# A decoder block on one core: pooling tiles behind all pairs' tiles, and an output projection in eight banks

## The chip, the cores and the metric

The kernel runs on one core of a Trainium2 chip. The metric is the device time of one execution in microseconds. A core has five engines with a queue each: TensorE (PE, matmuls; its weight loads are counted apart as PEld), VectorE (DVE), ScalarE (ACT), GpSimd (POOL), and SyncE (SP), which here issues every transfer between memory and the core. Matmuls write to PSUM, which has eight banks; one bank holds one 128x512 float32 tile.

## The reference

One decoder block on x of 512 tokens by 2048 channels. An adaLN vector (`mod`, six parts of 2048) shifts, scales and gates each half.

```
mod = silu(c) @ w_ada + b_ada                       # 6 x 2048
h   = rmsnorm(x) * (1 + sc1) + sh1
p   = h @ w_in                                      # 3360 RWKV columns + 1024 pooling columns
y_rwkv = rwkv7(p[:, :3360])                         # 16 heads of 64: r, k, v, decay, rate, gate
y_pool = pooling(p[:, 3360:])                       # 4 groups of 256, causal windows 2, 4, 8, 16, then a 256x256 matrix
x = x + gt1 * (concat(y_rwkv, y_pool) @ w_out)
x = x + gt2 * conv_ffn(rmsnorm(x) * (1 + sc2) + sh2)
out = rmsnorm(x)
```

In the pooling group with window w, each channel becomes its mean over the last w tokens minus itself, and the group's 256 channels are then mixed by one matrix. RWKV is a scan over tokens with a 64x64 state for each head.

## The kernel before

**Layout and tiles.** Activations lie transposed: 128 channels on the partitions, 512 tokens along the row. A product with a weight matrix is made of output tiles of 128 channels. For one tile, `project` (L122) loads the weights in blocks of 128x512 (four contraction steps of 128), splits each block into a high part (ACT, L112) and a low part (DVE, L114) and runs three matmuls for a step: high by high, high by low, low by high (`mm3`, L117; the profile's L118, L119, L120). A whole tile is 16 steps, 48 matmuls of 512 columns, accumulated in one PSUM bank. The activations are split in the same way into `ah` and `al` (`slots`, 16 pairs of homes); H, the first norm's output, lives in them, and later the 16 mixer outputs M.

**Stages.** First the norm and the first eight columns' tiles are built, while the first third of the adaLN rows is read. Then four quads follow, each two pairs of heads (four heads) of the RWKV mixer: `front(g)` (decay, rates, norm of k) and `rest(g)` (chunked scan: scores, a triangular inverse, eight chunk steps, group norm, gate). A quad is a long chain of small steps on PE, DVE and ACT, written under `hp()`, a higher priority. Around them stands the work that is to fill PE: `win_tile(fi)`, the remaining 27 tiles of the input projection. `win_pair(p, at)` makes the three tiles r, k and v of one pair, mixes each with its shifted self (`shift`, L232 and L233) and spills them to memory as `sp`; the quad loads them again (L693) when it starts. The tiles of the pooling columns (u tiles, two to a group) are spilled as `su` (L678 to L680).

**Order.** WIN_ORDER (L49) lays out the weights: three adaptor tiles, pairs 0 and 1, pairs 2 to 5, the eight pooling tiles, pairs 6 and 7. Pairs 2 and 3 are made under quad 0, pairs 4 and 5 under quad 1, the pooling tiles and pairs 6 and 7 under quad 2. Pooling itself (`pool(gi)`, L276), four groups in the order POOLS, is written behind quad 2 and has the high priority.

**Homes.** The order on each engine and the waits are set by a scheduler, by priority, by readiness in its own model of time, and by the homes of tiles. A tile name with one or two buffers is handed out again when its last user is done. Pooling borrows homes of the quads: K for the padded input, EM and EP for the running sums, INV for the result, AL for the output, and `war` (two buffers) for the pooling matrix. `war` is otherwise the home of the adaLN rows: `ada_rest` (L336) loads 96 blocks of 512 KB and multiplies each with silu(c) on DVE (L344), 24 written behind each quad. PSUM in this part: `mm` two banks (tiles and pooling), `bt` two by two banks and `ch` two banks (quads).

**Output projection.** Under quad 3 the first ten output tiles (NW) are made over the first 14 (NM) of 16 contraction steps: MIX_ORDER (L57) puts the eight pooling outputs first, then quads 0 to 2. The result, gated and added to x (L728), goes to memory as `part`. When quad 3 is done, all PSUM and working memory of this part are given back, and eight banks `b` are taken. `part` is loaded as x2 (L793), and the last two steps, quad 3's outputs, are added for the ten tiles. The six other tiles are made in two halves of 256 tokens each (`out_half`, L800), with the second norm behind them. The gated MLP follows; the change does not touch it.

The lines around the quads that the prediction speaks of:

Of the kernel before, what the change touches and what calls it, by code (L numbers as in the profile page):

```python
# [9 lines left out]
F32 = mybir.dt.float32  # L10
# [36 lines left out]

POOLS = (3, 1, 2, 0)
WIN_ORDER = ["T0", "T1", "T2", "r0", "k0", "v0", "r1", "k1", "v1"]  # L49
for _p in range(2, 6):  # L50
    WIN_ORDER += [f"r{_p}", f"k{_p}", f"v{_p}"]
WIN_ORDER += [f"u{2 * _g + _i}" for _g in POOLS for _i in range(2)]
for _p in range(6, NP):
    WIN_ORDER += [f"r{_p}", f"k{_p}", f"v{_p}"]


MIX_ORDER = [8 + 2 * _g + _i for _g in POOLS for _i in range(2)] + [0, 1, 2, 3, 4, 5, 6, 7]  # L57
NM = 14


# [1 line left out]
def block_kernel(ctx, tc, a, out, stop=None, dbg=None):  # L62
# [25 lines left out]
    def cols(name, lo, hi):  # L88
        return vec[:, COLS[name] + lo : COLS[name] + hi]
# [86 lines left out]
    if True:  # L176
# [53 lines left out]
        if True:  # L230
# [7 lines left out]
            def cell(tag, name):  # L238
                return ra.tile([P, WID.get(tag, 2 * T)], F32, tag=tag, name=name)

            def two(t):
                return t[:, 0 : 2 * T].rearrange("p (x t) -> p x t", x=2)
# [64 lines left out]
    def mmtile():  # L307
        return psa.tile([P, T], F32, tag="mm", name="mm", bufs=2)
# [7 lines left out]
    def win_tile(fi):  # L316
        ps = mmtile()
        project(ps, a["win1"][fi - 8, :, :], H)
        return ps
# [45 lines left out]
    def front(g, rkv):  # L365
        r, k, v = rkv
        lws = []
        for x in range(2):
            lw = ra.tile([P, 3, P], F32, tag="lw", name="lw", bufs=2)
            nc.sync.dma_start(lw, a["lora"][2 * g + x, :, :, :])  # L370
            lws.append(lw)

        def c2(name, x):
            return col(name, 2 * g + x)

        psw, psal = batch(), batch()
        for x in range(2):
            for m in range(2):
                PE.matmul(psw[HS[m], x, :], lws[x][0:64, 0, HS[m]], xwa[0:64, :], start=True, stop=True)
                PE.matmul(psal[HS[m], x, :], lws[x][64:128, 0, HS[m]], xwa[64:128, :], start=True, stop=True)  # L380
        sg = cell("EM", "sg")
        for x in range(2):
            S.activation(lead(sg)[:, NK * x : NK * x + NK, 1:], psw[:, x, :].rearrange("p (c t) -> p c t", t=C),
                         AF.Sigmoid, bias=c2("w0", x))
        V.memset(lead(sg)[:, :, 0:1], 0.0)
        al = cell("AL", "al")
        for x in range(2):
            act = S.activation(two(al)[:, x, :], psal[:, x, :], AF.Sigmoid, bias=c2("a0", x))
        with tc.issue_after(act.ins):
            act = S.preload_act_table_set("natural_log_exp_and_others")  # L390
        n = 2 * NK * (C + 1)
        V.tensor_tensor_scan(sg[:, 0:n], scanm[:, :, :].rearrange("p c t -> p (c t)"), sg[:, 0:n], 0.0,
                             op0=ALU.mult, op1=ALU.add)
        cs = lead(sg)
        mid = ra.tile([P, 2 * NK, 1], F32, tag="mid", name="mid")
        V.tensor_copy(mid, cs[:, :, C // 2 : C // 2 + 1])
        V.tensor_sub(cs, cs, mid[:, :, :].to_broadcast([P, 2 * NK, C + 1]))
        ep = cell("EP", "ep")
        em = sg
        fdec = ra.tile([P, 2 * NK, 1], F32, tag="fdec", name="fdec", bufs=2)  # L400
        with tc.issue_after(act.ins):
            S.activation(ep[:, 0:n], sg[:, 0:n], AF.Exp, scale=-Q)
            S.activation(em[:, 0:n], sg[:, 0:n], AF.Exp, scale=Q)
        V.tensor_mul(fdec[:, 0 : 2 * NK - 1], lead(ep)[:, 0 : 2 * NK - 1, C : C + 1], lead(em)[:, 1 : 2 * NK, 0:1])


        inv = cell("INV", "inv")
        psn = batch()
        for x in range(2):
            S.activation(two(inv)[:, x, :], two(k)[:, x, :], AF.Square, scale=c2("kk", x))  # L410
            PE.matmul(psn[:, x, :], bones, two(inv)[:, x, :], start=True, stop=True)
        V.tensor_scalar_max(flat(inv), wide(psn), 1e-24)
        with tc.issue_after(act.ins):
            S.activation(flat(inv), flat(inv), AF.Ln)
            S.activation(flat(inv), flat(inv), AF.Exp, scale=-0.5)
        for x in range(2):
            V.scalar_tensor_tensor(two(inv)[:, x, :], two(k)[:, x, :], c2("kk", x), two(inv)[:, x, :],
                                   op0=ALU.mult, op1=ALU.mult)
        return lws, al, ep, em, inv, fdec

    def rest(g, rkv, fr):
        r, k, v = rkv
# [234 lines left out]
    def win_pair(p, at):  # L657
        for i in range(3):
            ps = win_tile(at + i)
            t = ra.tile([P, T], F32, tag="spill", name="spill", bufs=2)  # L660
            shift(ps, 8 * i + p, t)
            d = tc.dram_tile([P, T], F32, name=f"sp{p}_{i}")
            nc.sync.dma_start(d, t)
            sp[p, i] = d

    def hp():
        return tc.high_priority(offset=100000)

    shift(win_tile(8), 17, two(rkv0[2])[:, 1, :])
    edge = []  # L670
    for g in range(NQ):
        if g < NQ - 1:
            if g == 2:
                for n, gi in enumerate(POOLS):
                    for i in range(2):
                        ps = win_tile(21 + 2 * n + i)
                        t = ra.tile([P, T], F32, tag="spill", name="spill", bufs=2)
                        S.copy(t, ps)  # L678
                        d = tc.dram_tile([P, T], F32, name=f"su{gi}_{i}")
                        nc.sync.dma_start(d, t)  # L680
                        su[gi, i] = d
            at = (9, 15, 29)[g]
            win_pair(2 * g + 2, at)
            win_pair(2 * g + 3, at + 3)
        with hp(), ExitStack() as after:
            for i in edge:
                after.enter_context(tc.issue_after(i.ins))
            rkv = rkv0
            if g:
                rkv = [cell(n, n.lower()) for n in RKV]  # L690
                for i in (1, 0, 2):
                    for x in range(2):
                        nc.sync.dma_start(two(rkv[i])[:, x, :], sp[2 * g + x, i])  # L693
            fr = front(g, rkv)
        with hp():
            rest(g, rkv, fr)
            if g == 2:
                for gi in POOLS:
                    edge = pool(gi)
        ada_rest(24 * g, 24 * g + 24)  # L700
        if g == 2:
            V.tensor_add(mod[:, 32:48], modq[:, 0, 0:16], modq[:, 1, 0:16])
            V.tensor_add(mod[:, 32:48], mod[:, 32:48], cols("b_ada", 32, 48))

    V.tensor_add(mod[:, 48:80], modq[:, 0, 16:48], modq[:, 1, 16:48])
    V.tensor_add(mod[:, 48:80], mod[:, 48:80], cols("b_ada", 48, 80))
    V.scalar_tensor_tensor(gsc2, mod[:, 64:80], 1.0, cols("n2", 0, 16), op0=ALU.add, op1=ALU.mult)


# [4 lines left out]
    def load_mix(i):  # L714
        t = wp.tile([P, WC], F32, tag="wraw", name="mxl", bufs=4)
        nc.sync.dma_start(t, mixd[MIX_ORDER[i]])
        M.append(split_act(i, t))

    for i in range(NM):
        load_mix(i)  # L720
    part = []
    for f in range(NW):
        if f % 2 == 0:
            xt = two(cell("K" if f % 4 == 0 else "R", "xt"))
            nc.sync.dma_start(xt, a["xT"][:, f : f + 2, :])
        ps = mmtile()
        project(ps, a["wout"][f, :, 0 : NM * P], M)
        V.scalar_tensor_tensor(xt[:, f % 2, :], ps, mod[:, 32 + f : 33 + f], xt[:, f % 2, :], op0=ALU.mult, op1=ALU.add)  # L728
        d = tc.dram_tile([P, T], F32, name=f"part{f}")
        nc.sync.dma_start(d, xt[:, f % 2, :])  # L730
        part.append(d)
    M += last_mix
    psctx.close()
    actx.close()

# [25 lines left out]
    def residual(f, ps, gate, acc, lo, hi, fresh):  # L761

        V.scalar_tensor_tensor(x2[f][:, lo:hi], ps, gate, x2[f][:, lo:hi], op0=ALU.mult, op1=ALU.add)
        sumsq(acc, x2[f][:, lo:hi], lo, hi, fresh)
# [22 lines left out]
            mm3(ups[i][:, hs], wh[:, sl], wl[:, sl], H2[k][0][:, hs], H2[k][1][:, hs], start=k == 0, stop=k == KT - 1)  # L787

    acc = rb.tile([P, T], F32, tag="acc", name="acc")
    x2 = []  # L790
    for f in range(KT):
        t = rb.tile([P, T], F32, tag=f"x2_{f}", name=f"x2_{f}")
        nc.sync.dma_start(t, part[f] if f < NW else a["xT"][:, f, :])  # L793
        x2.append(t)
    for f in range(NW):
        ps = bank()
        project(ps, a["wout"][f, :, NM * P :], M[NM:])
        residual(f, ps, mod[:, 32 + f : 33 + f], acc, 0, T, f == 0)

    def out_half(hf, f, engs=(V,)):  # L800
        ps = bank()[:, 0:HT]
# [225 lines left out]
```

## Time and profile before

| | |
|---|---|
| median of 3 runs | 2434.46 us |
| lowest, highest | 2431.72, 2441.41 us |
| profiled execution | 2428.03 us, span 2426.3 us |
| mean granted TensorE clock | 0.977 of full |
| PE, PEld busy | 2250.7 us (93%), 1825.1 us (75%) |
| DVE, ACT, POOL busy | 1344.6 us (55%), 817.7 us (34%), 27.3 us (1%) |
| moved | 357.05 MB, mean 147 GB/s |

The profile is of one execution. Its page gives the busy time of each engine, the span in 40 slices of 60.7 us (a digit is the busy share in tenths), and the costliest groups of instructions. Besides the page, the trace answers questions: a table by stage, a timeline of instructions, the sync queue's transfers, and who waited for whom. PE's busy time is modelled and overlapping matmuls are counted once; a few per cent of the matmul records can be missing.

### The profile page before, as it was taken

What the parts mean: (1) busy time and instruction counts of PE and PEld (TensorE: products, weight loads), DVE (VectorE), ACT (ScalarE), POOL (GpSimd) and SP (SyncE); (2) the same over time, 40 slices, a digit from 0 to 9 for tenths busy, and PEclk for the clock granted to TensorE, in tenths of its full rate; (3) what the DMA queues carried; (4) which work ended last, traced back from release to release, by engine and by line L of the source; (5) the groups of instructions that cost most, each with busy time, mean ns of one, the idle gap of its engine ahead of it and who ended that gap; (6) DMA issues with size and microseconds to landing.
All of it is one profiled execution on the core that took longest, in us unless ns stands there. A gap on an engine that the chain in (4) does not pass through costs nothing.

```text
span 2426.3 us, 36875 instructions
## 1 busy us (share of the span) xinstructions
PE 2250.7 (93%) x14434; PEld 1825.1 (75%) x14434; DVE 1344.6 (55%) x2230; ACT 817.7 (34%) x1349; POOL 27.3 (1%) x30
## 2 busy tenths in 40 slices
PE   4778899899857989999999999999999999999997
PEld 3656666678545779887888888888888888888887
DVE  7987784642496558657444433444344434444457
ACT  3242343332322346533223322333233323323333
POOL 0000000000000003000000000000000000000000
PEclk9989999999979999999999999999999999999998
DMA  9956762323577556447432333223322332332235
GB/s 358 339 208 209 239 190 82 96 89 122 188 237 247 179 200 202 144 156 256 127 99 97 96 97 99 96 96 96 99 96 97 97 98 96 96 100 96 96 101 174
DMA packets 186497, 357.05 MB, mean 147 GB/s; under 512 B 36305, under 2 KB 45265, under 8 KB 182097
## 3 DMA queue, kind: packets, MB, share of 16 engines
q1 hardware_dynamic: 186322, 354.69, 45.7%
q8 instruction: 113, 1.85, 0.3%
q14 instruction: 62, 0.51, 0.1%
HBM read 336.25 MB, written 18.36 MB: 146 GB/s over the span
## 4 chain that ended last, share of the span: by engine, by line
PE 74%; DVE 11%; DMA 9%; issue 3%; ACT 2%; SPq 1%; DVEq 0%; POOL 0%; ACTq 0%
PE b L118 20%; PE b L120 20%; PE b L119 20%; DMA war<-ada 4%; PE mm L120 4%; PE mm L118 4%; PE mm L119 3%; DVE jk L211 3%; DVE war L344 2%; DMA slot<-ada 1%; DVE wlo L114 1%; DMA wraw<-wup 1%; PE mm L298 1%; PE bt L561 0%; ACT ah L147 0%
## 5 line engine op out<-in xcount | busy, mean ns | idle before, releaser
L114 DVE TENSOR_TENSOR wlo<-wraw,whi 128x512 fp32r<-128x512 f32 (+1 forms) x782 | 534.9, 685 | 717.7 <-ACT whi L112 710.9
L112 ACT CAST whi<-wraw 128x512 fp32r<-128x512 f32 (+1 forms) x798 | 491.0, 616 | 1275.4 <-PE b L119 923.4
L120 PE MATMUL b<-hh,wlo 128*128 128x512 f32 (+1 forms) x1472 | 560.7, 381 | 7.2 <-DVE wlo L114 6.9
L118 PE MATMUL b<-hh,whi 128*128 128x512 f32 (+1 forms) x1472 | 559.9, 380 | 0.0
L119 PE MATMUL b<-hl,whi 128*128 128x512 f32 (+1 forms) x1472 | 559.6, 380 | 0.0
L118 PE MATMUL b<-ah,whi 128*128 128x512 f32 (+1 forms) x980 | 350.0, 357 | 4.5 <-ACT whi L112 3.5
L120 PE MATMUL b<-ah,wlo 128*128 128x512 f32 (+1 forms) x980 | 348.7, 356 | 4.7 <-DVE wlo L114 4.7
L119 PE MATMUL b<-al,whi 128*128 128x512 f32 (+1 forms) x980 | 348.5, 356 | 0.0
L120 PEld LDWEIGHTS b<-hh,wlo 128*128 128x128 f32 x1472 | 277.0, 188 | 62.6 <-DVE wlo L114 9.4
L118 PEld LDWEIGHTS b<-hh,whi 128*128 128x128 f32 x1472 | 277.1, 188 | 52.6 <-ACT whi L112 0.5
L119 PEld LDWEIGHTS b<-hl,whi 128*128 128x128 f32 x1472 | 277.1, 188 | 52.4
L118 PE MATMUL mm<-ah,whi 128*128 128x512 f32 x572 | 232.3, 406 | 10.7 <-ACT whi L112 10.7
L120 PE MATMUL mm<-ah,wlo 128*128 128x512 f32 x572 | 232.2, 406 | 4.9 <-DVE wlo L114 4.9
L119 PE MATMUL mm<-al,whi 128*128 128x512 f32 x572 | 230.2, 402 | 0.0
L118 PEld LDWEIGHTS b<-ah,whi 128*128 128x128 f32 x980 | 186.0, 190 | 34.1 <-ACT whi L112 6.0
L120 PEld LDWEIGHTS b<-ah,wlo 128*128 128x128 f32 x980 | 186.0, 190 | 31.4 <-DVE wlo L114 5.8
L119 PEld LDWEIGHTS b<-al,whi 128*128 128x128 f32 x980 | 186.1, 190 | 26.9 <-DVE al L141 1.2
L344 DVE SCALAR_TENSOR_TENSOR war<-war,cq 128x1024 f32<-128x1024 f32 x96 | 117.0, 1222 | 54.6 <-DMA war<-ada 53.9
L118 PEld LDWEIGHTS mm<-ah,whi 128*128 128x128 f32 x572 | 109.1, 191 | 38.7 <-ACT whi L112 11.5
L120 PEld LDWEIGHTS mm<-ah,wlo 128*128 128x128 f32 x572 | 109.0, 191 | 33.9 <-DVE wlo L114 8.9
L119 PEld LDWEIGHTS mm<-al,whi 128*128 128x128 f32 x572 | 109.1, 191 | 24.3 <-issue 1.7
L889 DVE SCALAR_TENSOR_TENSOR x<-b,mod,x 128x512 f32<-128x512 f32 x80 | 59.7, 751 | 111.7 <-PE b L120 111.7
(223 smaller groups left out, 1733.2 us busy)
## 6 DMA issues: line engine op xcount, KB each, us to landing
wraw<-wup SPq DMA_DIRECT2D x368, 256.0 KB, 3.0
war<-ada SPq DMA_DIRECT2D x96, 512.0 KB, 4.4
wraw<-wdn SPq DMA_DIRECT2D x192, 256.0 KB, 2.7
wraw<-win SPq DMA_DIRECT2D x140, 256.0 KB, 3.5
wa<-ada SPq DMA_DIRECT2D x32, 1024.0 KB, 7.1
wraw<-wout SPq DMA_DIRECT2D x78, 256.0 KB, 3.5
slot<-ada SPq DMA_DIRECT2D x64, 256.0 KB, 3.6
sp<-spill SPq DMA_DIRECT2D x18, 256.0 KB, 3.3
```

The lines of the kernel that those rows point to most:

```text
L112: S.copy(hi[:, 0:w], raw[:, 0:w])
L114: eng.tensor_tensor(lo[:, 0:w], raw[:, 0:w], hi[:, 0:w].bitcast(F32), op=ALU.subtract)
L118: PE.matmul(ps, wh, xh, start=start, stop=False)
L119: PE.matmul(ps, wh, xl, start=False, stop=False)
L120: return PE.matmul(ps, wl, xh, start=False, stop=stop)
L211: V.scalar_tensor_tensor(jk, wa, 1.0, cb, op0=ALU.mult, op1=ALU.mult, accum_out=mod[:, j : j + 1])
L298: pe = PE.matmul(ps, pw[:, i, d * P : (d + 1) * P], z[:, i, :], start=i == 0, stop=i == 1)
L344: V.scalar_tensor_tensor(wa, wa, 1.0, cq[0], op0=ALU.mult, op1=ALU.mult, accum_out=modq[:, kq, j : j + 1])
L889: V.scalar_tensor_tensor(x2[f], ps, mod[:, 80 + f : 81 + f], x2[f], op0=ALU.mult, op1=ALU.add)
```

## The change

- WIN_ORDER: the pairs 2 to 7 come first, the eight pooling tiles last. MIX_ORDER: quads 0 to 2, pooling, quad 3.
- Pairs 6 and 7 are made under quad 2; the pooling tiles under quad 3.
- `pool` is written behind quad 3's `rest`, with the order that it is issued behind the last load of quad 3's inputs and behind the last step of quad 3's `front`. The wait of a quad on pooling (`edge`) is dropped, and the inputs are loaded in the order r, v, k instead of k, r, v.
- The adaLN rows are summed once, for all of `mod[:, 32:80]`, behind the last quad.
- The partial output projection with its `part` tiles is dropped. When the eight banks are there, eight output tiles are made side by side in four blocks of four steps each (`out_block`); x is loaded as x2 during the third block row; the residuals follow; tiles 8 and 9 are made whole.

```diff
-for _p in range(2, 6):
+for _p in range(2, NP):
     WIN_ORDER += [f"r{_p}", f"k{_p}", f"v{_p}"]
 WIN_ORDER += [f"u{2 * _g + _i}" for _g in POOLS for _i in range(2)]
-for _p in range(6, NP):
-    WIN_ORDER += [f"r{_p}", f"k{_p}", f"v{_p}"]
-MIX_ORDER = [8 + 2 * _g + _i for _g in POOLS for _i in range(2)] + [0, 1, 2, 3, 4, 5, 6, 7]
+MIX_ORDER = [0, 1, 2, 3, 4, 5] + [8 + 2 * _g + _i for _g in POOLS for _i in range(2)] + [6, 7]
...
     for g in range(NQ):
         if g < NQ - 1:
-            if g == 2:
-                for n, gi in enumerate(POOLS):
-                    for i in range(2):
-                        ps = win_tile(21 + 2 * n + i)
-                        ...
-            at = (9, 15, 29)[g]
-            win_pair(2 * g + 2, at)
-            win_pair(2 * g + 3, at + 3)
-        with hp(), ExitStack() as after:
-            for i in edge:
-                after.enter_context(tc.issue_after(i.ins))
+            win_pair(2 * g + 2, 9 + 6 * g)
+            win_pair(2 * g + 3, 12 + 6 * g)
+        else:
+            for n, gi in enumerate(POOLS):
+                for i in range(2):
+                    ps = win_tile(27 + 2 * n + i)
+                    t = ra.tile([P, T], F32, tag="spill", name="spill", bufs=2)
+                    S.copy(t, ps)
+                    d = tc.dram_tile([P, T], F32, name=f"su{gi}_{i}")
+                    nc.sync.dma_start(d, t)
+                    su[gi, i] = d
+        with hp():
             rkv = rkv0
             if g:
                 rkv = [cell(n, n.lower()) for n in RKV]
-                for i in (1, 0, 2):
+                for i in (0, 2, 1):
                     for x in range(2):
-                        nc.sync.dma_start(two(rkv[i])[:, x, :], sp[2 * g + x, i])
-            fr = front(g, rkv)
-        with hp():
+                        load = nc.sync.dma_start(two(rkv[i])[:, x, :], sp[2 * g + x, i])
+            fr, norm = front(g, rkv)
             rest(g, rkv, fr)
-            if g == 2:
-                for gi in POOLS:
-                    edge = pool(gi)
+            if g == NQ - 1:
+                with tc.issue_after(load.ins), tc.issue_after(norm.ins):
+                    for gi in POOLS:
+                        pool(gi)
         ada_rest(24 * g, 24 * g + 24)
...
-    for i in range(NM):
-        load_mix(i)
-    part = []
-    for f in range(NW):
-        ...
-        project(ps, a["wout"][f, :, 0 : NM * P], M)
-        V.scalar_tensor_tensor(xt[:, f % 2, :], ps, mod[:, 32 + f : 33 + f], xt[:, f % 2, :], op0=ALU.mult, op1=ALU.add)
-        ...
-        part.append(d)
-    M += last_mix
     psctx.close()
     actx.close()
...
+    def out_block(f, k0):
+        return project(pss[f], a["wout"][f, :, k0 * P : (k0 + 4) * P], M[k0 : k0 + 4], start=k0 == 0, stop=k0 == KT - 4)
+
     x2 = []
-    for f in range(KT):
-        t = rb.tile([P, T], F32, tag=f"x2_{f}", name=f"x2_{f}")
-        nc.sync.dma_start(t, part[f] if f < NW else a["xT"][:, f, :])
-        x2.append(t)
-    for f in range(NW):
+    pss = [bank() for _ in range(8)]
+    for k0 in range(0, KT, 4):
+        for i in range(k0, min(k0 + 4, NM)):
+            load_mix(i)
+        if k0 == KT - 4:
+            M += last_mix
+        for f in range(8):
+            out_block(f, k0)
+            if k0 == 8:
+                for i in range(2):
+                    t = rb.tile([P, T], F32, tag=f"x2_{2 * f + i}", name=f"x2_{2 * f + i}")
+                    nc.sync.dma_start(t, a["xT"][:, 2 * f + i, :])
+                    x2.append(t)
+    for f in range(8):
+        residual(f, pss[f], mod[:, 32 + f : 33 + f], acc, 0, T, f == 0)
+    for f in range(8, NW):
         ps = bank()
-        project(ps, a["wout"][f, :, NM * P :], M[NM:])
-        residual(f, ps, mod[:, 32 + f : 33 + f], acc, 0, T, f == 0)
+        project(ps, a["wout"][f, :, :], M)
+        residual(f, ps, mod[:, 32 + f : 33 + f], acc, 0, T, False)
```

More of the change, by code (lines that the diff above doesn't have):

```diff
@@ L416, in front @@
         for x in range(2):
-            V.scalar_tensor_tensor(two(inv)[:, x, :], two(k)[:, x, :], c2("kk", x), two(inv)[:, x, :],
-                                   op0=ALU.mult, op1=ALU.mult)
-        return lws, al, ep, em, inv, fdec
+            norm = V.scalar_tensor_tensor(two(inv)[:, x, :], two(k)[:, x, :], c2("kk", x), two(inv)[:, x, :],
+                                          op0=ALU.mult, op1=ALU.mult)
+        return (lws, al, ep, em, inv, fdec), norm
     def rest(g, rkv, fr):
@@ L669, in block_kernel @@
     shift(win_tile(8), 17, two(rkv0[2])[:, 1, :])
-    edge = []
     for g in range(NQ):
         if g < NQ - 1:
-            if g == 2:
-                for n, gi in enumerate(POOLS):
-                    for i in range(2):
-                        ps = win_tile(21 + 2 * n + i)
[L677 to L681, printed above, removed]
-            at = (9, 15, 29)[g]
-            win_pair(2 * g + 2, at)
-            win_pair(2 * g + 3, at + 3)
-        with hp(), ExitStack() as after:
-            for i in edge:
-                after.enter_context(tc.issue_after(i.ins))
+            win_pair(2 * g + 2, 9 + 6 * g)
[10 more added lines that the diff above has]
+        with hp():
             rkv = rkv0
@@ L690, in block_kernel @@
                 rkv = [cell(n, n.lower()) for n in RKV]
-                for i in (1, 0, 2):
+                for i in (0, 2, 1):
                     for x in range(2):
-                        nc.sync.dma_start(two(rkv[i])[:, x, :], sp[2 * g + x, i])
-            fr = front(g, rkv)
-        with hp():
+                        load = nc.sync.dma_start(two(rkv[i])[:, x, :], sp[2 * g + x, i])
+            fr, norm = front(g, rkv)
             rest(g, rkv, fr)
-            if g == 2:
-                for gi in POOLS:
-                    edge = pool(gi)
+            if g == NQ - 1:
+                with tc.issue_after(load.ins), tc.issue_after(norm.ins):
+                    for gi in POOLS:
+                        pool(gi)
         ada_rest(24 * g, 24 * g + 24)
[L701 to L706, printed above, removed]
+    V.tensor_add(mod[:, 32:80], modq[:, 0, :], modq[:, 1, :])
+    V.tensor_add(mod[:, 32:80], mod[:, 32:80], cols("b_ada", 32, 80))
     V.scalar_tensor_tensor(gsc2, mod[:, 64:80], 1.0, cols("n2", 0, 16), op0=ALU.add, op1=ALU.mult)
@@ L717, in load_mix @@
         M.append(split_act(i, t))
-    for i in range(NM):
-        load_mix(i)
-    part = []
-    for f in range(NW):
[L723 to L726, printed above, removed]
-        project(ps, a["wout"][f, :, 0 : NM * P], M)
-        V.scalar_tensor_tensor(xt[:, f % 2, :], ps, mod[:, 32 + f : 33 + f], xt[:, f % 2, :], op0=ALU.mult, op1=ALU.add)
-        d = tc.dram_tile([P, T], F32, name=f"part{f}")
-        nc.sync.dma_start(d, xt[:, f % 2, :])
-        part.append(d)
-    M += last_mix
     psctx.close()
```

## The prediction

> **What bounds the kernel now.** I read the page first: its head and its slices.
>
> ```profile
> span 2426.3 us, 36875 instructions
> PE   4778899899857989999999999999999999999997
> ```
>
> TensorE (PE) is full but for the first slices and the 5 and the 7 in the middle (667 to 788 us, at 60.7 us a slice). So I asked for the stages from quad 2 on. The columns: stage, length, busy us of PE, weight load, DVE, ACT, POOL, granted clock, DMA share, GB/s.
>
> ```profile
> 420.50:541.00 120.50, 110.53 (x1513) 81.89 (x1513) 69.55 (x123) 45.34 (x76) 0.95 (x1) 0.99 0.31 92
> 541.00:645.50 104.50, 103.83 (x440) 81.95 (x439) 34.35 (x50) 30.12 (x49) 0.00 (x0) 1.00 0.42 136
> 645.50:712.00 66.50, 30.24 (x368) 17.79 (x369) 52.17 (x92) 25.00 (x34) 0.00 (x0) 0.73 0.75 235
> 712.00:807.00 95.00, 82.32 (x1085) 62.09 (x1084) 68.52 (x131) 24.93 (x50) 0.00 (x0) 0.92 0.80 252
> 807.00:857.00 50.00, 48.87 (x215) 39.81 (x213) 19.59 (x37) 12.48 (x24) 0.00 (x0) 1.00 0.41 130
> ```
>
> Under quad 2 (first row) projection tiles fill PE. From 541 to 645.5 it does nothing but tiles: quad 3 waits for its inputs, which the order puts last. From 645.5 to 712 the tiles are gone and PE is busy 30.24 of 66.50 us, at a clock of 0.73: quad 3's front and half of its rest run bare. The timelines (start, length, engine, line) date this.
>
> ```profile
> 532.52 1.22 DVE L648 TENSOR_TENSOR rs<-rs,bt 128x1024 f32<-128x1024 f32 x1
> 539.51 0.58 ACT L678 COPY spill<-mm 128x512 f32<-128x512 f32 x1
> 550.39 0.58 ACT L678 COPY spill<-mm 128x512 f32<-128x512 f32 x1
> 626.55 0.68 ACT L232 ACTIVATE spill<-mm,drv 128x512 f32<-128x512 f32 x1
> 644.90 0.68 ACT L232 ACTIVATE spill<-mm,drv 128x512 f32<-128x512 f32 x1
> 652.54 0.80 SPq L693 DMA_DIRECT2D k<-sp  x2
> 662.68 1.27 ACT L383 ACTIVATE sg<-bt,vec 128x512 f32<-128x512 f32 x2
> ```
>
> Quad 2 ends at 532.5; quad 3 runs from 662.7 to 806.2. A tile alone takes 550.39 - 539.51 = 10.88 us. At 539.5 eighteen tiles are done (v1, the 12 of pairs 2 to 5, five pooling tiles).
>
> **The war loads** (adaLN rows: a 512 KB load, then a 1.2 us DVE product, L344) slow a quad. The stages of quads 0, 2 and 3, first whole, then L344 alone (two records to a load; quad 2 has none):
>
> ```profile
> 165.85:303.50 137.65, 119.07 (x1528) 88.17 (x1529) 103.78 (x190) 46.24 (x77) 0.96 (x1) 0.97 0.70 220
> 422.55:533.80 111.25, 101.28 (x1474) 74.83 (x1472) 63.27 (x116) 41.23 (x71) 0.95 (x1) 0.98 0.30 87
> 662.68:806.20 143.52, 99.50 (x1415) 74.78 (x1416) 112.87 (x208) 43.16 (x74) 0.00 (x0) 0.85 0.79 247
> 165.85:303.50 137.65, 46.70 (x76) 0.97 0.70 220
> 662.68:806.20 143.52, 54.12 (x89) 0.85 0.79 247
> ```
>
> Quad 0 with 38 loads takes 26 us more than quad 2 with none, quad 3 with 45 takes 32: 0.70 us for each load. The sync queue tells why the last 48 fall on quad 3:
>
> ```profile
> 344.74 0.33 SPq L343 DMA_DIRECT2D war<-ada  x1
> 346.67 0.33 SPq L270 DMA_DIRECT2D pw<-poolw  x1
> 349.55 0.33 SPq L270 DMA_DIRECT2D pw<-poolw  x1
> 649.70 0.33 SPq L343 DMA_DIRECT2D war<-ada  x1
> ```
>
> Pool weights share the two war buffers. Buffers go out in the order of the code, so two pool weights sat in both from 347 to 650. By the same rule quad 3's K came only at 652.5, behind the last pooling group's pad.
>
> **The change, step by step.**
>
> Step 1, order. Nothing is added to PE: 27 input tiles and ten whole output tiles stay. Pairs 6 and 7 become tiles 14 to 19. At 539.5 + 10.88 the 19th is done instead of the last at 645, and K and the other homes no longer stand behind the pool. Quad 3 can follow quad 2.
>
> Step 2, war. The next 24 loads are now in the code ahead of the pool weights, so they follow the first 48 from 350 on, under quads 1 and 2. Price 24 x 0.70 = 17 us of quad, in which PE still does some 0.85 tile (quad 2's pace is below), 9 us. Cost 8, ends 0 and 17.
>
> Step 3, quad 3 under eight pooling tiles. Matmuls on mm in quad 2's stage and in the pure stage:
>
> ```profile
> 422.55:533.80 111.25, 66.01 (x254) 45.27 (x252) 0.74 (x1) 3.01 (x5) 0.98 0.30 87
> 541.00:645.50 104.50, 103.83 (x440) 81.95 (x439) 3.72 (x5) 8.87 (x13) 1.00 0.42 136
> ```
>
> 104.5 us hold 9.6 tiles or 461 matmuls, of which 440 are on record; so 254 are 266, 5.5 tiles, 60 us. A quad under tiles costs PE 111 - 60 = 51 us. Its sg can come near 556: k7, the 18th tile, near 545, then spill, store and load, 10 us as from K's load (652.54) to sg now. From 541 PE has one tile, eight pooling tiles and a quad: 541 + 9 x 10.88 + 51 + 8 = 698. The quad ends near 670, its war loads being gone; some three pooling tiles run alone after it. The order r, v, k of its loads may start it up to 10 us later; tiles fill that, so it costs nothing unless tiles run out.
>
> Step 4, pooling. Its matmuls take mm homes after the last tile has taken one, so they start when the seventh is evacuated, as they did at 628:
>
> ```profile
> 628.09 1.98 PE L298 MATMUL mm<-z,pw 128*128 128x512 f32 x4
> 652.62 6.71 PE L298 MATMUL mm<-z,pw 128*128 128x512 f32 x8 [2.95 <-issue]
> 659.37 0.78 ACT L300 ACTIVATE mxp<-mm,drv,vec 128x512 f32<-128x512 f32 x1 [2.13 <-PE mm L298]
> 857.56 0.47 PE L118 MATMUL b<-ah,whi 128*128 128x512 f32 x1 [0.94 <-DVE xt L728]
> 871.67 0.80 PE L120 MATMUL b<-ah,wlo 128*128 128x512 f32 x1 [3.89 <-DVE wlo L114]
> 872.26 0.63 PE L118 MATMUL b<-ah,whi 128*128 128x512 f32 x1
> 872.69 0.63 PE L119 MATMUL b<-al,whi 128*128 128x512 f32 x1
> 880.77 0.28 PE L118 MATMUL b<-ah,whi 128*128 128x256 f32 x1
> ```
>
> They then took 32 us, to 660.1, one group behind the other through single homes. From 688 that ends at 720; beside it the eighth tile ends near 705, and its round trip through memory into the last group fits (ready about 714). What covers the tail of 15 us? Output blocks on the six banks that the quad has left could; but at 857.56 the first output tile waited for the evacuation of the last mm tile, though quad 3's banks had been idle for 50 us. So I let the first block wait for pooling: start 721, ends 706 and 730.
>
> Step 5, output. Ten tiles, 108.8 us: 721 to 830. Removed: ten 128x256 weight splits (the 14 + 2 cut makes five a tile, now four), ten stores and loads of part, ten DVE steps at L728: hidden work, worth nothing by itself. The burst of 16 x2 loads, behind which weight loads stood (the wait at 871.67), becomes two loads a block:
>
> ```profile
> 860.30 4.97 SPq L793 DMA_DIRECT2D x<-part  x10
> 865.31 3.83 SPq L793 DMA_DIRECT2D x<-xT  x6
> ```
>
> The mixes' splits lie under the eighth tile and the blocks. The last two mixes need the homes of H 14 and 15, so quad 3's last ACT step now waits for the eighth tile; weight casts would queue behind it if it is placed too early, up to one tile, 11 us; I take 0. POOL's queue is untouched.
>
> Step 6, the last 24 war loads. They stand behind the pool weights, so they start near 710, beside the blocks, and all residuals now need all 96. Rate in quad 3: 45 in 143.5 us, 3.2 us each: done at 787. The first residual is due at 721 + 25 x 2.72 = 789, and the bank is needed at 808. Data in that time:
>
> ```profile
> war<-ada SPq DMA_DIRECT2D x96, 512.0 KB, 4.4
> wraw<-wout SPq DMA_DIRECT2D x78, 256.0 KB, 3.5
> mxl<-mixd SPq DMA_DIRECT2D x14, 256.0 KB, 3.7
> x<-xT SPq DMA_DIRECT2D x6, 256.0 KB, 5.4
> 0.00:50.00 50.00, 18.71 (x66) 14.05 (x67) 34.73 (x55) 20.94 (x31) 1.39 (x9) 1.00 0.96 363
> ```
>
> 24 war, 32 weight, 14 mix and 16 x loads are 28.9 MB, to pass in 97 us (711 to 808). At the 252 GB/s of 712 to 807 that is 115 us, 18 too many; at the first stage's 363, 80, none. 252 was moved at a share of 0.80, which full would be 315: 92 us, enough. I take 5 for DVE standing at late loads, ends 0 and 18. The Trainium skill, DMA: Bandwidth & Descriptors (Specifications), gives an HBM limit of about 358 GB/s for a core; the first stage agrees with its 363, and by that figure alone the term would be 0.
>
> The sum: 830 + 5 = 835, where the first half-column tile (128x256) would start, against 880.8 now. All behind it is unchanged. Gain 46; the blocks filling the tail would add 15. The profiled execution is 2428.03, 0.3% under the median 2434.46: 2382 on its scale, 2388 on the median's, which I say.
>
> The Trainium skill, TensorE: Matmul & The Clock Gate (Part 1), says that an idle window of about 3.4 us halves the clock until a busy one has passed. The spacing after the 3.89 us wait agrees (872.69 - 872.26 = 0.43, against 10.88 / 48 = 0.23), and it speaks against the bare tail of step 4: one or two slow windows there, at 1.7 us each.
>
> **Rivals.**
> A. The blocks fill the tail, or the war stretch is free: against it stands the row 857.56, for it the six idle banks. 820 or less, gain 60 to 75: 2360 to 2374.
> B. Output held by data: war loads late, DVE standing in front of weight splits, PE waiting in pieces. For it: the 54.12 us of L344 under quad 3; against it: the 807 to 857 row, full speed without war. Costs 18 to 40: gain 8 to 30, 2404 to 2426.
> C. The gain goes elsewhere: quad 3 gets through, but pooling and output start as late as now, say because quad 3's last step holds up ACT. Within 12 us of 2434.
> D. Slower. Quad 3 starts only behind the pooling tiles, because its loads sit on the sync queue behind a spill. Tiles end at 541 + 98 + 8 = 647, sg comes at 657, then the quad runs bare with the last war loads, 111 + 17, to 785, and no output runs beside it, as its banks are the quad's: 785 + 109 + 5 = 899, 18 later than now, 2453. It decides where sg + 128 + 114 passes 880.8: sg after 639, 83 us past my 556. Against it: in this profile sg comes 10 us after K's load.
>
> **How the numbers follow.** My forecast (gain 30 to 60) 0.64, A 0.10, B 0.15, C 0.06, D 0.05. Range 2362 to 2416: it leaves out the end of A, the end of B, C and D. 0.5%, 12 us, is about what a measurement can tell. Faster 0.88 (forecast, A, nearly all of B), same 0.07, slower 0.05.
>
> **What would show it.** Quad 3's sg (L383) near 556 instead of 662.7; 48 L344 records between 350 and 450; no stage like 645.5 to 712; the first b block about 15 us behind the eighth pooling tile; the first half-column tile near 835. I am wrong if sg comes after 600, if the first residual waits for mod, or if PE is under 90% busy in the blocks.

## The result, and the profile after

| | before | changed |
|---|---|---|
| median | 2436.82 us (4 runs) | 2410.23 us (4 runs, 2404.25 to 2413.24) |
| profiled execution, span | 2428.03, 2426.3 us | 2404.25, 2402.5 us |

The ratio is 0.9888 [0.9859, 0.9917], a gain of 26.6 us; a second measurement, beside the kernel before on another chip, gave 0.989 [0.9873, 0.9906]. The range on record (2362 to 2416) holds the time, and the sign is right. But the likeliest case promised a gain of 30 to 60: what came lies in rival B's 8 to 30, and its interval, 20 to 34 us, only reaches into the likeliest case. The first half-column tile, whose start the sum gave, was put at 835; it went from 880.77 to 854.42.

The page after: span, and PE's busy tenths and granted clock over 40 slices of 60 us.

```profile
span 2402.5 us, 36790 instructions
PE   4778898999988999999999999999999999999997
PEclk9989999999999999999999999999999999999999
```

The 5 and the 7 of the middle are gone, and with them the stage in which quad 3 ran bare. Two eights (the twelfth and thirteenth slice, about 660 to 780 us) are left there. The same stages as a table, in the columns used before (stage, length, PE, weight load, DVE, ACT, POOL, clock, DMA share, GB/s): pooling, then the output blocks in three parts.

```profile
691.93:730.26 38.33, 26.71 (x77) 14.31 (x76) 19.35 (x31) 12.21 (x19) 0.00 (x0) 0.87 0.65 206
730.26:760.00 29.74, 28.96 (x125) 23.36 (x126) 19.51 (x33) 7.27 (x12) 0.00 (x0) 1.00 0.84 269
760.00:790.00 30.00, 19.88 (x78) 15.24 (x77) 21.26 (x34) 6.82 (x11) 0.00 (x0) 0.81 0.89 286
790.00:854.42 64.42, 64.42 (x281) 53.16 (x280) 30.61 (x48) 21.93 (x36) 0.00 (x0) 0.98 0.52 181
```

Pooling loses 11.6 us of PE, and the blocks lose 10.1 in the one stage from 760 to 790. The timeline gives the places that the prediction dated; the brackets are idle time before the instruction and what ended it.

```profile
551.23 1.27 ACT L381 ACTIVATE sg<-bt,vec 128x512 f32<-128x512 f32 x2
557.54 0.32 SPq L687 DMA_DIRECT2D k<-sp  x1
665.64 1.22 DVE L646 TENSOR_TENSOR rs<-rs,bt 128x1024 f32<-128x1024 f32 x1
691.30 0.58 ACT L677 COPY spill<-mm 128x512 f32<-128x512 f32 x1
710.70 0.58 ACT L677 COPY spill<-mm 128x512 f32<-128x512 f32 x1
724.05 5.34 PE L296 MATMUL mm<-z,pw 128*128 128x512 f32 x8 [9.52 <-issue]
730.26 0.50 PE L116 MATMUL b<-ah,whi 128*128 128x512 f32 x1 [0.87 <-ACT mxp L298]
786.15 0.80 PE L116 MATMUL b<-ah,whi 128*128 128x512 f32 x1 [10.12 <-ACT whi L110]
786.74 0.63 PE L117 MATMUL b<-al,whi 128*128 128x512 f32 x1
787.17 0.63 PE L118 MATMUL b<-ah,wlo 128*128 128x512 f32 x1
854.42 0.28 PE L116 MATMUL b<-ah,whi 128*128 128x256 f32 x1
```

Quad 3 follows quad 2 at once (sg at 551, its end at 666). The seventh and eighth pooling tiles are evacuated at 691 and 711. Then PE stands for 9.5 us. The row names no releaser (`issue`), but the last pooling group's round trip lies in that time: the store is issued at 712.5, the load at 716.5, and DVE's running sums are done at 723.95. After that the first block waits for the evacuation of pooling's last result. In the blocks PE stands once for long, 10.12 us, for the high part of a weight block, and runs at about half speed behind that wait (0.43 us from matmul to matmul, against 10.88 / 48 = 0.23). The Trainium skill, TensorE: Matmul & The Clock Gate (Part 1), lets an idle window of some 3.4 us halve the clock; the row agrees.

The weight block was late because its load was issued late. The sync queue in those microseconds:

```profile
778.31 0.33 SPq L341 DMA_DIRECT2D war<-ada  x1
778.73 0.39 SPq L707 DMA_DIRECT2D mxl<-mixd  x1
781.12 0.33 SPq L341 DMA_DIRECT2D war<-ada  x1
781.54 0.38 SPq L108 DMA_DIRECT2D wraw<-wout  x1
```

And what that queue waited for from 705 to 800 (us in total, times, longest):

```profile
SPq L341 <- DVE war L342: 47.0, 22, 4.5
```

Between every two mixes or weights of this stretch stands a war load that waits until DVE has released a war buffer. Read alone, this says that the order on the queue costs the 10 us. An experiment below takes that order away and gains nothing.

### The profile page after: what moved, and what is told of

Read it like the earlier page. It is cut to its first block, busy times and chain, and to the rows that moved or that the text cites. A ratio compares the mean times of both kernels' runs of the same rounds, so it can differ in the third digit from the quotient of the medians.

```text
span 2402.5 us, 36790 instructions
## 1 busy us (share of the span) xinstructions
PE 2247.2 (94%) x14434; PEld 1819.8 (76%) x14434; DVE 1338.7 (56%) x2208; ACT 815.5 (34%) x1339; POOL 27.2 (1%) x30
## 4 chain that ended last, share of the span: by engine, by line
PE 71%; DMA 12%; DVE 11%; issue 3%; ACT 2%; SPq 1%; DVEq 0%; POOL 0%; ACTq 0%; POOLq 0%
PE b L116 21%; PE b L118 21%; PE b L117 21%; DMA war<-ada 5%; DVE jk L209 3%; PE mm L118 2%; PE mm L116 2%; PE mm L117 2%; DVE war L342 1%; DVE wlo L112 1%; DMA slot<-ada 1%; DMA wraw<-wup 1%; DMA wraw<-win 1%; DMA upad<-su 1%; DMA dxy<-xyl 0%
## 5 line engine op out<-in xcount | busy, mean ns | idle before, releaser
L110 ACT CAST whi<-wraw 128x512 fp32r<-128x512 f32 x788 | 489.1, 622 | 1253.4 <-PE b L117 959.6
L112 DVE TENSOR_TENSOR wlo<-wraw,whi 128x512 fp32r<-128x512 f32 x772 | 533.3, 692 | 665.8 <-ACT whi L110 657.4
L116 PE MATMUL b<-ah,whi 128*128 128x512 f32 (+1 forms) x1120 | 405.2, 362 | 15.7 <-ACT whi L110 12.8
L118 PE MATMUL b<-ah,wlo 128*128 128x512 f32 (+1 forms) x1120 | 403.8, 361 | 0.8 <-DVE wlo L112 0.8
L117 PE MATMUL b<-al,whi 128*128 128x512 f32 (+1 forms) x1120 | 403.4, 360 | 0.0
L116 PEld LDWEIGHTS b<-ah,whi 128*128 128x128 f32 x1120 | 212.5, 190 | 51.6 <-ACT whi L110 14.3
L118 PEld LDWEIGHTS b<-ah,wlo 128*128 128x128 f32 x1120 | 212.6, 190 | 33.5 <-DVE wlo L112 2.5
L118 PE MATMUL mm<-ah,wlo 128*128 128x512 f32 x432 | 179.3, 415 | 3.9 <-DVE wlo L112 3.9
L116 PE MATMUL mm<-ah,whi 128*128 128x512 f32 x432 | 178.3, 413 | 1.7 <-ACT whi L110 1.7
L117 PE MATMUL mm<-al,whi 128*128 128x512 f32 x432 | 176.5, 409 | 0.4 <-issue 0.4
```

What stands on the lines that cost most here:

```text
L110: S.copy(hi[:, 0:w], raw[:, 0:w])
L112: eng.tensor_tensor(lo[:, 0:w], raw[:, 0:w], hi[:, 0:w].bitcast(F32), op=ALU.subtract)
L116: PE.matmul(ps, wh, xh, start=start, stop=False)
L117: PE.matmul(ps, wh, xl, start=False, stop=False)
L118: return PE.matmul(ps, wl, xh, start=False, stop=stop)
```

## The experiments

Each was timed beside the kernel before on the same chip; edits are against the changed kernel unless said otherwise. The first block and the first half-column tile, called start and end of the blocks, are the gauge.

**The war loads beside the blocks.** The last 24 were left out (their part of adaLN is zero).

```diff
+    G.memset(modq, 0.0)
...
-        ada_rest(24 * g, 24 * g + 24)
+        if g < NQ - 1:
+            ada_rest(24 * g, 24 * g + 24)
```

> The last 24 war loads and their products are left out (that part of adaLN is zero); pool weights stay in the war buffers. Theory 'war': the wait near 775 goes, blocks run at 2.72 us, the first half-column tile comes at 836 to 842, 13 to 18 us under the changed kernel. Rival 'homes': the wait stays, 0 to 4 us. In both, the first block still waits for pooling (near 727 to 730).

2389.28 us, 0.9821 [0.9807, 0.9834]. Start and end of the blocks:

```profile
731.57 0.50 PE L116 MATMUL b<-ah,whi 128*128 128x512 f32 x1 [0.87 <-ACT mxp L298]
840.51 0.28 PE L116 MATMUL b<-ah,whi 128*128 128x256 f32 x1
```

108.94 us without a wait, where step 5 had 108.8. So the war loads beside the blocks cost 124.16 - 108.94 = 15.2 us, and without them the blocks lose nothing. A second traced execution of the changed kernel took 124.14 us here, with one wait of 10.98.

**Order on the queue, or data and DVE?** The last 24 war loads were issued from GpSimd's queue: the same bytes, products and homes, but no mix or weight stands behind them.

```diff
-            nc.sync.dma_start(wa, a["ada2"][kq, j, :, :])
+            (nc.gpsimd if n >= 72 else nc.sync).dma_start(wa, a["ada2"][kq, j, :, :])
```

> The changed kernel; the last 24 adaLN row loads are issued from GpSimd's queue instead of the sync queue, all else alike. The same bytes, the same DVE products, the same two homes. Theory (order on the sync queue: war loads that wait for DVE's release stand ahead of mixes and weights): the 47 us of sync-queue waits of line 341 on DVE go, the 10.1 us PE wait near 776 goes, the first block to the first half-column tile falls from 124.2 to 109 to 114 us, 10 to 15 us less than the changed kernel, ratio to before 0.983 to 0.985. Rival (data rate, or DVE's 24 products standing in front of the weight splits): the same bytes and products still lie beside the blocks, so 119 to 125 us, ratio 0.987 to 0.990.

2411.43 us, 0.9913 [0.9897, 0.9929]: no gain. Start and end of the blocks:

```profile
734.92 0.50 PE L116 MATMUL b<-ah,whi 128*128 128x512 f32 x1 [0.87 <-ACT mxp L298]
862.98 0.28 PE L116 MATMUL b<-ah,whi 128*128 128x256 f32 x1
```

The queue's 47 us behind war are gone, and the blocks take 128.06 us, 3.9 more than with them. So the order on the sync queue is not by itself the cost: with it away, as much is lost elsewhere. The trace shows where. PE now waits six times for a low split of DVE, 7.4 us in all. Each time a war product that had waited for its load stands ahead of that split on DVE. The longest of the six, for a block whose high part was done at 777.1:

```profile
778.88 1.23 DVE L342 SCALAR_TENSOR_TENSOR war<-war,cq 128x1024 f32<-128x1024 f32 x1 [1.21 <-DMA war<-ada]
780.03 0.69 DVE L112 TENSOR_TENSOR wlo<-wraw,whi 128x512 fp32r<-128x512 f32 x1
780.78 0.80 PE L118 MATMUL b<-ah,wlo 128*128 128x512 f32 x1 [2.90 <-DVE wlo L112]
```

A seventh wait, 4.85 us at 817.4, hangs on a mix whose load was issued at 810.6, behind 16 x loads. One order has made room for two others, DVE's and that of the x loads. Nor is the swap clean: GpSimd's issue may have a price of its own. All 96 loads issued there cost some 34 us in a run below, and a gain from the order may be hidden behind such a price here.

The stage from 730 to 790, first in the changed kernel:

```profile
730.00:790.00 60.00, 48.84 (x201) 38.61 (x202) 41.02 (x66) 14.30 (x24) 0.00 (x0) 0.91 0.86 277
```

Then with the loads on GpSimd's queue:

```profile
730.00:790.00 60.00, 54.10 (x211) 40.05 (x210) 36.46 (x61) 15.98 (x26) 10.34 (x20) 0.95 0.82 264
```

And without the last war loads:

```profile
730.00:790.00 60.00, 59.13 (x260) 48.38 (x259) 21.03 (x31) 19.79 (x32) 0.00 (x0) 1.00 0.61 205
```

What goes with the 15 us is the war work itself, from whichever queue: 59 to 72 GB/s more, the DMA engines' share 0.82 to 0.86 instead of 0.61, and DVE busy 36 to 41 us instead of 21. Loads also land later: the mixes of this stage (256 KB each) in 4.4 us from issue, the median of 8, in the changed kernel, and in 3.0, the median of 10, without the last war loads.

Are the data the cost? The rate of the changed kernel from 711 to 802:

```profile
711.00:802.00 91.00, 69.70 (x265) 51.71 (x266) 52.60 (x85) 19.96 (x32) 0.00 (x0) 0.87 0.83 270
```

At 270 GB/s step 6's bytes (28.8 MB; it rounded to 28.9) take 107 us where it had 97: 10 too many, about the wait seen. But 270 is not a ceiling. The version that fills the tail, further below, moved more in the stretch from 730 to 790, with loads of the same kinds:

```profile
730.00:790.00 60.00, 49.27 (x208) 39.27 (x207) 43.15 (x71) 15.44 (x25) 0.00 (x0) 0.91 0.91 300
```

At 300 GB/s the bytes take 96 us, within the 97 there were, and PE still waited 16.2 us for weights in that version. So data alone are not shown to be the cost. How the 15.2 us divide between data, DVE's 24 products ahead of the low splits, the order on the queues and the few homes that mixes and weights share stays open. The next run was to test the homes.

**Homes of the mixes.** The mixes got two homes of their own (the expectation speaks of four).

```diff
-        t = wp.tile([P, WC], F32, tag="wraw", name="mxl", bufs=4)
+        t = rb.tile([P, T], F32, tag="t0", name="mxl", bufs=2)
```

> The mixes are loaded into four homes of their own (those of the later conv tiles) instead of the four raw weight buffers; war untouched. Theory 'war on the sync queue': the loads still pass one queue behind war loads that wait for DVE, so the wait near 775 stays or only moves, 0 to 4 us. Rival 'homes': weights can be loaded ahead while mixes land; the wait goes and the time falls by 8 to 12 us against the changed kernel.

2450.74 us, 1.0082 [1.0066, 1.0097], and it answers another question. The last 20 war loads, the first mix load and the first block:

```profile
728.84 53.85 SPq L341 DMA_DIRECT2D war<-ada  x20
782.74 0.90 SPq L707 DMA_DIRECT2D mxl<-mixd  x2
787.72 0.80 PE L116 MATMUL b<-ah,whi 128*128 128x512 f32 x1 [62.44 <-ACT ah L138]
```

The new homes lie in the working memory that is taken when the old one is given back, and there the mixes came to stand on the sync queue behind all war loads: the first was issued at 782.7, directly behind the last of them. The x loads of the changed kernel lie in the same memory and come late too, the first at 789.6, 3.5 us behind the last war load, against 731.9 in the run without the last 24. Which release they wait for the profile does not say. Whether separate homes would help stays open.

**War under the quads.** Only the first 48 war loads were made; beside the run without the last 24, this prices the 24 between.

```diff
+    G.memset(modq, 0.0)
...
-        ada_rest(24 * g, 24 * g + 24)
+        if g < 2:
+            ada_rest(24 * g, 24 * g + 24)
```

> Only the first 48 war loads are made (the other 48 and their products are left out, that part of adaLN is zero); pool weights in the war buffers. Against e2, which makes 72, it prices the 24 loads under quads 1 and 2. The prediction took 8 us with ends 0 and 17. In the changed kernel the 19th tile was done at 566.3 where 550.4 was expected without war: by that 12 to 16 us, quad 3's sg at 536 to 541, first half-column tile at 825 to 829. If only 8, sg near 545 and the half-column tile at 832.

2375.56 us, 0.976 [0.9738, 0.9782], 13.7 us below the run with 72. The end of quad 1 and the start of the blocks:

```profile
421.93 1.22 DVE L647 TENSOR_TENSOR rs<-rs,bt 128x1024 f32<-128x1024 f32 x1
717.95 0.50 PE L116 MATMUL b<-ah,whi 128*128 128x512 f32 x1 [0.87 <-ACT mxp L298]
```

The end of quad 1 in the changed kernel, whose loads up to there are those of the run with 72:

```profile
447.94 1.22 DVE L646 TENSOR_TENSOR rs<-rs,bt 128x1024 f32<-128x1024 f32 x1
```

All 24 lie under quad 1: their products run from 356.5 to 435.1 us in the changed kernel. They hold its end up by 26 us (28 in the run with 72, where it came at 449.92), some 1.1 us a load. Tiles fill half of that, and the blocks start 731.57 - 717.95 = 13.6 us earlier without them.

**The last war loads earlier.** The pool weights got homes of the quad, so that no war load stands behind pooling.

```diff
-        t = ra.tile([P, 2 * T], F32, tag="war", name="pw", bufs=2)
+        t = cell("Y" if gi in (3, 2) else "PM", "pw")
```

> The pool weights go to two homes of the quad (Y and PM) instead of the war buffers, so that all 96 war loads follow each other from the start. Theory 'war': in the changed kernel the last 24 war loads stand on the sync queue, in the transfers and in DVE's order in front of the mixes and weights of the output blocks; the 10 us wait of PE near 775 goes, the first half-column tile (854.4 us in the changed kernel) comes near 842, and the time is 8 to 13 us under the changed kernel (2410 to about 2400); quads 1 to 3 take 0.7 us more for each load that moves under them, which tiles cover in part. Rival 'homes': the mixes share the four raw weight buffers with the weights, and PE waits for that, whatever war does: the wait near 775 stays and the time is the changed kernel's or up to 8 us over it.

2397.38 us, 0.9859 [0.9843, 0.9875]. Start and end of the blocks:

```profile
737.37 0.50 PE L116 MATMUL b<-ah,whi 128*128 128x512 f32 x1 [0.87 <-ACT mxp L298]
846.32 0.28 PE L116 MATMUL b<-ah,whi 128*128 128x256 f32 x1
```

The blocks take 108.95 us again and start 7.1 later: under quad 2 (products from 440 to 541) the 24 loads cost about half of their price beside the blocks. Quad 2 itself grew by 24 us, from 103.2 to 127.1 between quad 1's end and its own, nearly as much as quad 1 had. Tiles fill more of the delay here. No war load was left out. The gain over the changed kernel, some 7 us, is at the edge of what the intervals of the two tell apart.

**The tail.** Six of the eight tiles took the quads' banks, two the `mm` banks; the old PSUM is given back behind the eight residuals.

```diff
-    psctx.close()
...
-    pss = [bank() for _ in range(8)]
+    pss = []
+    for pair in (batch(), batch(), chain()):
+        pss += [pair[:, 0, :], pair[:, 1, :]]
+    pss += [mmtile(), mmtile()]
...
+    psctx.close()
...
```

> The eight output tiles take the quads' own PSUM homes (bt, bt, ch, then the two mm), in the same PSUM pool, so that six of them need not wait for pooling's mm homes; the rest as in the changed kernel. Theory 'banks': the 19 us between the end of the last pooling tile (711) and the first block (730) are a wait for mm homes; the first block comes near 713, and the time falls by 10 to 16 us. Theory 'war' alone: the blocks start earlier but then run into the war loads, which start no earlier, so most of it is given back in the second and third row: 0 to 6 us.

2406.9 us, 0.9879 [0.986, 0.9898], the changed kernel's own ratio. Two of the five executions took 2397 us and three 2407; the trace is of one of the two. Start and end of the blocks:

```profile
712.17 0.80 PE L116 MATMUL bt<-ah,whi 128*128 128x512 f32 x1
849.43 0.28 PE L116 MATMUL b<-ah,whi 128*128 128x256 f32 x1
```

PE's largest wait from 640 to 860:

```profile
PE bt L116 <- ACT whi L110: 16.2, 3, 9.7
```

Even there the blocks, which start 18.1 us earlier, into the tail, end only 5.0 earlier: the rest went, in the main, into waits for weights. While war lies beside the blocks, PE time gained ahead of them is lost in them.

**Both.** The two edits above together.

> Both edits: pool weights in quad homes, output tiles in the quads' PSUM homes. If war and banks are separate costs, the gains add: 20 to 27 us under the changed kernel, first half-column tile at 827 to 834. If they are one cost seen twice, the gain is that of the larger alone, 10 to 15 us.

2386.53 us, 0.9813 [0.9799, 0.9826], the fastest version with all the work in it, and clear of the changed kernel's 0.9859 to 0.9917. Start and end of the blocks:

```profile
721.80 0.80 PE L116 MATMUL bt<-ah,whi 128*128 128x512 f32 x1
836.01 0.28 PE L116 MATMUL b<-ah,whi 128*128 128x256 f32 x1
```

The stage between:

```profile
740.00:836.00 96.00, 95.06 (x420) 78.41 (x419) 40.25 (x60) 31.59 (x53) 0.00 (x0) 1.00 0.48 163
```

PE is busy 95.06 of 96 us. The end is 18.4 us ahead of the changed kernel's and 10.3 ahead of the version that only moves the pool weights: the tail's gain counts once war is away.

**The order alone.** The new order, with the old split projection over 14 mixes and its `part`; the gates of the attention half are summed behind quad 2's war loads, as they were.

```diff
...
+    for i in range(NM):
+        load_mix(i)
+    part = []
+    for f in range(NW):
...
+        project(ps, a["wout"][f, :, 0 : NM * P], M)
...
-    pss = [bank() for _ in range(8)]
-    for k0 in range(0, KT, 4):
...
-            out_block(f, k0)
...
+        project(ps, a["wout"][f, :, NM * P :], M[NM:])
...
```

> The new order of tiles, quads and pooling with the old projection: ten tiles over 14 steps in mm, stored as part, the last two steps in the eight banks (the gate third of mod is summed early again, as before). Theory 'order': the gain is the order's, the eight banks are worth little: 5 to 12 us slower than the changed kernel (the first tile needs all mixes at once, and the burst of x2 loads comes back), ratio to before 0.991 to 0.994. Rival 'banks': the unsplit projection carries half of the gain or more: ratio 0.995 or more.

2428.55 us, 0.9981 [0.9968, 0.9994]. The first output matmul:

```profile
745.54 0.80 PE L116 MATMUL mm<-ah,whi 128*128 128x512 f32 x1 [15.88 <-ACT whi L110]
```

**The banks alone.** The old order and mix order, with the eight-bank projection.

```diff
-for _p in range(2, NP):
+for _p in range(2, 6):
...
-MIX_ORDER = [0, 1, 2, 3, 4, 5] + [8 + 2 * _g + _i for _g in POOLS for _i in range(2)] + [6, 7]
+MIX_ORDER = [8 + 2 * _g + _i for _g in POOLS for _i in range(2)] + [0, 1, 2, 3, 4, 5, 6, 7]
...
-            if g == NQ - 1:
-                with tc.issue_after(load.ins), tc.issue_after(norm.ins):
-                    for gi in POOLS:
-                        pool(gi)
+            if g == 2:
+                for gi in POOLS:
+                    edge = pool(gi)
...
```

> The old order with the new projection in eight banks: quad 3 keeps its place behind all tiles, and the output has to wait for its banks. Theory 'order': the projection's first 95 us, which stood beside quad 3, come behind it: the first half-column tile moves from 880.8 to 915 to 925, 35 to 45 us slower than before (ratio 1.014 to 1.019). Rival 'banks': eight banks are a gain by themselves: ratio at or under 1.0.

2456.12 us, 1.0102 [1.0087, 1.0118]. Quad 3's stage:

```profile
700.00:750.00 50.00, 18.55 (x492) 16.30 (x484) 35.20 (x74) 1.90 (x2) 0.00 (x0) 0.66 0.64 196
```

The start of the blocks:

```profile
791.66 0.39 PE L118 MATMUL b<-ah,whi 128*128 128x512 f32 x1
```

On their chip, with the kernel before at 2432.46, the order is worth 4 us, the banks cost 24, and both together gain 28.6 (2403.88). Neither part does it alone. With the old order there is nothing to run under quad 3 but the output, and the eight banks take it away (PE 18.55 of 50). With the new order the output comes behind pooling; partial tiles over all 14 mixes began 15 us later than the blocks do, and the last steps still come as a pass of their own.

**War work on other engines.** On the version with both edits, first all 96 products moved to GpSimd with the sums on ACT, then, with products back on DVE, all 96 loads issued from GpSimd.

```diff
-            V.scalar_tensor_tensor(wa, wa, 1.0, cq[0], op0=ALU.mult, op1=ALU.mult,
-                                   accum_out=modq[:, kq, j : j + 1])
+            G.tensor_mul(wa, wa, cq[0])
+            S.activation(wa, wa, AF.Copy, accum_out=modq[:, kq, j : j + 1])
```

> e7 (pool weights in quad homes, output tiles in the quads' PSUM homes) with the war product taken off DVE: GpSimd multiplies, ACT sums. Theory 'DVE in order': war costs a quad time because chain steps queue on DVE behind a product that waits for its load; then quads 0 to 2 get 15 to 30 us shorter, tiles fill less of them, and the time falls 6 to 15 us under e7 (2386.5). Rival 'transfers': the cost is the 512 KB loads in front of the quad's own small transfers; then within 4 us of e7. If GpSimd and DVE hinder each other in SBUF, it is slower than e7.

```diff
-            nc.sync.dma_start(wa, a["ada2"][kq, j, :, :])
+            nc.gpsimd.dma_start(wa, a["ada2"][kq, j, :, :])
```

> The version with pool weights in quad homes and blocks on the quads' banks (0.9813 to before); all 96 adaLN row loads are issued from GpSimd's queue. It asks what the 13.7 us are that the 24 loads under quads 1 and 2 cost. Theory that they too are order on the sync queue (weights and quad inputs behind a war load that waits): 10 to 25 us less, ratio 0.971 to 0.977. Rival that they are DVE's time (1.3 us a product ahead of the quad's own steps): no gain, 0.980 to 0.983; issuing from GpSimd may cost something of its own, above 0.983 if so.

2478.02 us, 1.0179 [1.0152, 1.0205], and 2421.17 us, 0.9951 [0.9934, 0.9968]: both lose to 0.9813. The stage from 200 to 400 us in the version with both edits:

```profile
200.00:400.00 200.00, 174.11 (x2161) 129.38 (x2160) 147.23 (x277) 60.92 (x100) 0.95 (x1) 0.95 0.72 225
```

With the products on GpSimd:

```profile
200.00:400.00 200.00, 157.79 (x1806) 115.62 (x1801) 113.17 (x163) 98.34 (x171) 98.21 (x42) 0.87 0.56 174
```

ACT's largest wait there, from 160 to 630:

```profile
ACT war L343 <- POOL war L342: 157.1, 74, 6.6
```

With the loads issued from GpSimd:

```profile
200.00:400.00 200.00, 161.02 (x1674) 117.17 (x1674) 143.79 (x277) 56.05 (x93) 30.00 (x56) 0.93 0.72 228
```

PE is busy 16 and 13 us less in these 200. With the product on GpSimd, ACT's sums wait for it 157 us, ahead of the weight casts in ACT's queue, so the run does not say what the order on DVE had cost. Why issuing from GpSimd slows the quads stays open, and so does what the price of a war load under a quad is made of.

## Why the prediction was right, and where its size was not

Start of the half-column tile: 834.8 by the sum, 854.4 measured. The 19.6 us between them lie in three places: 3.3 up to the seventh pooling tile, 6.0 from there to the first block, 10.4 in the blocks.

- **Step 1 held.** Quad 3 follows quad 2, and no stage like 645 to 712 is left. That the other homes go free with the pool was right. That sg came at 551 where step 3 had 556 is luck: the sum had it wait for k7, spilled, stored and loaded, but k7 was evacuated at 552.4 (said 545) and K's load issued at 557.5, both behind sg's start.
- **Step 2 was too small.** The 24 loads, which all came to lie under quad 1: 8 said (ends 0 and 17), 13.6 measured. The unit, 0.70 us a load, came from whole quads that also differ in other things; the run with 48 loads gave some 1.1. The share that PE fills, about half, was right.
- **Step 3 held**, and a little slack in it hid part of step 2: 666 for the quad's end (said 670), 691.3 for the seventh tile (said 688). Step 2 alone would have made that tile 5.6 us late; it was 3.3.
- **Step 4** had the mechanism (blocks wait for `mm`, not for the quad's banks: row 730.26) and the bare tail, but gave 33 us from the seventh tile to the first block, where 39.0 went by. The eighth tile beside the pooling chain came 19.4 us behind the seventh, not 17, and the tail behind it was 19.6, not 16, and in 9.5 of these PE stood, around the last group's round trip. That tail is no work of the last war loads: without them it was 18.7. 6.0 of the 19.6.
- **Step 5 held** to 0.2 us for the blocks (108.94 without the last war loads). It called the work taken out with the split "worth nothing by itself"; no run takes out that work alone. But the new order is worth 4 us with the split projection and 28.6 without it, so the gain needs the new projection as much as the order. ACT's last step of quad 3 (0 said) held PE 1.1 us.
- **Step 6 is the term that was most mis-sized.** It took 5 us between 0 and 18; the war loads cost 15.2. Its times came close: the last product was due to be done at 787 and began at 789.6. What failed is the choice within the range. The row of 252 GB/s at a share of 0.80 came from a like mix of work and gave 18; I scaled it to a full share (315 GB/s), called that enough, and left 5 for DVE. Over 711 to 802 the changed kernel moved 270. That is not to say that the rate made the loss: another version moved 300, and its PE waited too. Mixes and weights stand behind the war work on the sync queue, which the step does not name, and low splits stand behind it on DVE, for which it had the 5. 10.4 of the 19.6, on top of the 5.

The Trainium skill's 358 GB/s for a core (DMA: Bandwidth & Descriptors, Specifications) would have made this term 0. The stage moved 270 and PE did wait: the measurement decides, and a limit on the rate was no forecast of it.

**The signs.** None of the three signs of being wrong came: sg was at 551; the first residual, at 813.8, waited for PE, with `mod` done at 792.6; and PE was busy 113.25 of the blocks' 124.16 us, 91%, just over the 90% that was named. The first block came 19.6 us behind the eighth pooling tile, not about 15.

**The rivals.** B had the place right: PE waits in the blocks because the last war loads lie there, and low splits stand behind war products. Its size is in part luck. It priced the war loads at 18 to 40 us, and they cost 15.2; the gain of 26.6 falls in its 8 to 30 only because 9.3 us were lost ahead of the blocks. It had 0.15, and its evidence against, the 807 to 857 row at full speed, was from a stage without war. A failed as put: the blocks did not enter the tail. Where they were let in (0.9879) it brought nothing clear of the noise until war was away as well. C and D did not come: pooling and output start with the tiles' end, and sg was 88 us ahead of D's deciding 639.

## What to carry to other kernels

The price of work that can go anywhere depends on how much of the delay the bound engine can fill: 24 loads cost 15 us beside the output blocks, where PE had nothing else, 13.6 under quad 1 and 7 under quad 2, though each quad grew by 24 us or more. When a row shows what a like mixture of transfers did, be slow to scale it up to full use: here the 18 of the row was nearer to 15.2 than the 5 that was taken. And a queue in which loads visibly stand behind a waiting one shows an order, not yet a cost: take the waiting load out of it, and look where the bound engine waits then, before calling it the cause.

## What the runs showed of the hardware beyond that

DVE's low split of a 128x512 block grew when GpSimd multiplied beside it. The groups of instructions from 160 to 630 us (busy us, mean ns of one), with the war products on GpSimd:

```profile
L112 DVE TENSOR_TENSOR wlo<-wraw,whi 128x512 fp32r<-128x512 f32 x73 | 78.7, 1086 | 64.3 <-ACT whi L110 59.7 <-DMA wraw<-win 2.0 <-PE mm L118 1.4
```

In the version with both edits, products on DVE:

```profile
L112 DVE TENSOR_TENSOR wlo<-wraw,whi 128x512 fp32r<-128x512 f32 x91 | 62.2, 686 | 15.7 <-ACT whi L110 14.3 <-PE mm L118 1.1 <-ACT sf L592 0.3
```

1086 against 686 ns, in the same line of code. One pair of the run with the products on GpSimd shows how:

```profile
228.47 2.39 POOL L342 TENSOR_TENSOR war<-war,cq 128x1024 f32<-128x1024 f32 x1 [3.05 <-DMA war<-ada]
228.88 2.53 DVE L112 TENSOR_TENSOR wlo<-wraw,whi 128x512 fp32r<-128x512 f32 x1
```

The split began 0.41 us behind the product, took 2.53 us and ended 0.55 us behind it; the one before, with no product beside it, took 0.69 us. The Trainium skill, SBUF — State Buffer (SBUF: two separate sides), has DVE and GpSimd take turns at a shared port for a DVE step with two SBUF inputs; the rows agree. The 128x1024 product itself took 2.38 us (median) on GpSimd and 1.22 on DVE.
